# A four-layer encoder step in fp32: the first rows' projection by feature and unscaled, first weights on ScalarE's queue, the gain spread by matmuls

## The chip, the core and the metric

The kernel runs on one core of a Trainium2 chip. The metric is the device time of one execution in microseconds, given as the median of several runs; the profile is of one execution more. The core has TensorE (PE), VectorE (DVE), ScalarE (ACT), GpSimd (POOL) and SyncE (SP), which here issues the DMAs. Each engine takes its instructions in the order of the built program and waits on semaphores for the others.

## What is computed

One step of a small encoder: 512 prompt rows and 8 x 16 sample rows, so 640 rows of 1024 features, in two layers of mixer and SwiGLU. Only the first layer's beginning matters here. Its mixer starts with an RMS norm and a projection, and the columns `v` of that projection are layer-normalised:

```python
def rms_norm(x, g):
    y = x * rsqrt(mean(x * x, axis=-1) + EPS)
    return y * g
h = rms_norm(x, norm_mix_pre[0])
u, v, bg, cg, xb = split(h @ ev_w_in[0])          # five times 512 columns
vn = (v - mean(v)) * rsqrt(var(v) + EPS) * v_gain # chunk_mlp
s  = tril(W_s) @ vn + b;  ya = u * s
```

The factor `r = rsqrt(mean(x * x) + EPS)` is one number a row. So v can be projected from rows that carry only the gain g: it comes out divided by r, and its variance divided by r squared.

## The kernel before

The 640 rows are five tiles of 128 (t = 0 to 4; 4 holds the sample rows). A tile goes through these steps, of which the first four are `pre_norm` (L352) and `Quarters.take` (L317):

1. `load` (L1271 in `main`) brings the rows in, 512 KB.
2. ScalarE squares them and sums along the row, VectorE makes the mean, POOL takes the power -0.5 (`rsqrt`, L234), VectorE multiplies rows by r and by the gain tile (`SCALAR_TENSOR_TENSOR`). The gain tile is a 512 KB DMA that repeats one row in all 128 partitions (`bcast`, L200).
3. PE transposes the result: eight transposes of 128 x 128 (`flip`, L171) into two PSUM banks.
4. `take` splits the transposed tile into a high part (a cast to fp32r on ScalarE) and a low part (a subtraction on VectorE), copies of it (`f`, `a21`) to ScalarE, and the sums s1 to s4 that a later product scheme by quarters (Strassen's) needs. Tile 2 lies across the two halves and is also split into `mid`, here a `q` tile.
5. `v_proj` (L418): 24 products of 128 x 512 columns into one bank: eight k blocks, each high x high, high x low, low x high. The weights come in four loads of 512 KB (w0 to w3, `raw` tiles), each split by `operand` (L219) into a `q` tile by one cast and one subtraction of 1024 columns.
6. `v_evac` (L717): statistics of v on VectorE, r by POOL, and `vn` out of PSUM on ScalarE (`ACTIVATE vn<-ps`).

After the five tiles the mixer's other columns follow in `pairs` (L770); the first pair is done plainly (`PlainUnits`), with products of 128 x 320 columns.

All accumulators and transposes come from one pool of eight PSUM banks (`psp`, L159). A tile of this pool is written again as soon as the last reader of the one before it in its bank is done: for a pair of transposes these readers are the splits, the f copies and, for the tiles 2 to 4, the a21 copies.

What order the engines take is set in three ways. `Weave` (L48) runs the generators of the source by a clock of expected PE time, so waits written as numbers (`A1`, `A2`, the argument of `W.signal`) set the order in which instructions are written. `tc.high_priority()` marks the norm steps, so the scheduler of the tile framework draws them ahead. `Ordered` (L87) keeps ScalarE's and VectorE's instructions of the opening of `main` in program order. Each engine then runs its list strictly in order.

Of the kernel before, what the change touches and what calls it, by code (L numbers as in the profile page):

```python
# [35 lines left out]
A1 = 2000  # L36
A2 = 5000
# [68 lines left out]
def trunk_kernel(  # L106
# [48 lines left out]
    hidp = ctx.enter_context(tc.tile_pool(name="hidp", bufs=7))  # L155
# [6 lines left out]
    W = Weave()  # L162
# [25 lines left out]
    def st(n=1):  # L188
        return stp.tile([P, n], F32, tag="st", name=nm("st"))
# [16 lines left out]
    def raw():  # L206
        return rawp.tile([P, 5, 512], F32, tag="raw", name=nm("raw"))

    def fetch(srcs):

        for i, src in enumerate(srcs):
            if i % 2 == 0:
                w = raw()[:, :4, :].rearrange("p (h a) c -> p h (a c)", h=2)
                nc.sync.dma_start(out=w[:, 0, :], in_=src)
                if i + 1 < len(srcs):
                    nc.sync.dma_start(out=w[:, 1, :], in_=srcs[i + 1])
            yield w[:, i % 2, :]

    def operand(src):  # L219
        n = src.shape[-1]  # L220
        q = qp.tile([P, 2, D], F32R, tag="q", name=nm("q"))
        split((q[:, 0, :n], q[:, 1, :n]), src)
        return q
# [4 lines left out]
    def split(dst, val):  # L228
        act.copy(out=dst[0], in_=val)
        dve.tensor_tensor(out=dst[1], in0=val, in1=dst[0].bitcast(F32), op=ALU.subtract)  # L230

    def rsqrt(ms):
        r = st()
        nc.gpsimd.tensor_tensor(out=r, in0=ms, in1=mhalf, op=ALU.pow)  # L234
        return r
# [113 lines left out]
                split((self.s4[:, 0, :, o], self.s4[:, 1, :, o]), s4)  # L349
                W.signal(self.sum[t], 4500)  # L350

    def pre_norm(t, x, X, wait, xn=None):  # L352
        if xn is None:
            xn = t4([P, D])
        with tc.high_priority():
            norm = Norm()
            norm.add(x, xn)
            r = norm.get()
            dve.scalar_tensor_tensor(out=xn, in0=x, scalar=r, in1=X.gain, op0=ALU.mult, op1=ALU.mult)
        yield wait  # L360
        ps = []
        for half in range(2):
            ps.append(bank((P, HK, P)))
            for i in range(HK):
                k = HK * half + i
                flip(ps[half][:, i, :], xn[:, k * P : (k + 1) * P])
        yield 500
        X.take(t, ps)

# [45 lines left out]
                yield  # L415
        return ps[:, :n]

    def v_proj(X, hls, evac):  # L418
        for t in range(TT):
            for e in X.ready(t):  # L420
                yield e
            ps = bank()
            for k in range(NK):
                q = hls[k // 2][:, :, k % 2 * 512 : (k % 2 + 1) * 512]
                x = X.rows(k, t)
                mm(ps, x[0], q[:, 0, :], k == 0, False, 512)
                mm(ps, x[0], q[:, 1, :], False, False, 512)
                mm(ps, x[1], q[:, 0, :], False, k == NK - 1, 512)
                if k % 4 == 3:
                    yield  # L430
            evac(t, ps)
# [50 lines left out]
    def in_row(t):  # L482
        return xp[t * P : (t + 1) * P, :] if t < 4 else xs
# [224 lines left out]
        o = hist_n + NP  # L708
        return buf[:, o : o + NB * (hist_n + LS)].rearrange("p (b s) -> p b s", s=hist_n + LS)

    def even_mixer(X, hls):
        vn = {}
        vns = [hidp.tile([P, 2, NT], F32, tag="hid", name=nm("vn")) for _ in range(3)]
        consts = [t4([P, 2, 512]) for _ in range(2)]
# [2 lines left out]
        def v_evac(t, ps):  # L717
            stats = st(6)
            dve.bn_stats(out=stats, in_=ps)
            mv = st(2)  # L720
            dve.bn_aggr(out=mv, in_=stats)
            ve = st()
            dve.tensor_scalar(out=ve, in0=mv[:, 1:2], scalar1=EPS, scalar2=None, op0=ALU.add)
            r = rsqrt(ve)
            vn[t] = vns[t // 2][:, t % 2, :512]
            nm_ = st()
            dve.scalar_tensor_tensor(
                out=nm_, in0=mv[:, 0:1], scalar=-1.0, in1=r, op0=ALU.mult, op1=ALU.mult
            )
            act.activation(out=vn[t], in_=ps, func=AF.Identity, scale=r, bias=nm_)  # L730
            if t == 4:
                o = t2([P, 512])
                dve.tensor_tensor(out=o, in0=vn[t], in1=gn, op=ALU.mult)
                nc.sync.dma_start(out=nav, in_=o)
# [1 line left out]
        gn = bcast(v_gain[0], 512, lambda _: consts[0][:, 0, :])  # L736
        gcol = cst.tile([P, 4], F32, name="gcol")
        nc.sync.dma_start(out=gcol, in_=v_gain_t)
        yield from v_proj(X, hls, v_evac)
        W.signal(v_ready, 4000)  # L740

        wT = consts[1][:, 0, :].rearrange("p (g i) -> p g i", i=P)
# [3 lines left out]
        for b in range(NB):  # L746
            r = slice(b * LS, (b + 1) * LS)
            nc.sync.dma_start(out=wS[r, :, r], in_=sp_wT[0:LS, :, 0:LS])
        for g in range(4):
            for w in (wT, wS):  # L750
                nc.gpsimd.affine_select(  # L751
                    out=w[:, g, :],
                    in_=w[:, g, :],
# [509 lines left out]

    def main():
        X = Quarters(None, True)
        feed = fetch([ev_v[i] for i in range(4)])
        xt = []

        def load(t):
            xt.append(t4([P, D]))  # L1270
            nc.sync.dma_start(out=xt[t], in_=in_row(t))  # L1271

        def start(t, wait):
            g = pre_norm(t, xt[t], X, wait)
            next(g)
            W.spawn(g, 0, wait)

        Ordered.on = True
        load(0)
        X.gain = bcast(g_mix_pre[0], D, t4)  # L1280
        w = [next(feed) for _ in range(2)]
        load(1)
        w += [next(feed) for _ in range(2)]
        first = pre_norm(0, xt[0], X, 0)
        next(first)
        hls = [operand(w[0])]
        for _ in first:
            pass
        W.signal(X.top[0])
        hls.append(operand(w[1]))  # L1290
        start(1, A1)
        hls += [operand(w[2]), operand(w[3])]
        for t in range(2, TT):
            load(t)
            start(t, A1 + (t - 1) * A2)
        Ordered.on = False
        X = yield from even_mixer(X, hls)
        nxt = []

        def mid():  # L1300
            gpost = bcast(g_ffn_post[0], D, t4)
            nxt.append(Normed(bcast(g_mix_pre[1], D, t4)))
            return make_fin(gpost, x_row, x_row, nxt[0])

        yield from ffn(0, X, mid)
        X = yield from odd_mixer(nxt[0])

# [102 lines left out]
```

## Time and profile before

| | |
|---|---|
| time, median of 3 runs | 1320.69 us (1320.46 to 1320.77) |
| the profiled execution | 1320.24 us |
| its span on the core | 1318.5 us |
| PE busy | 1294.0 us, 98% |
| VectorE busy | 889.0 us, 67% |
| ScalarE busy | 614.0 us, 47% |
| first PE instruction | 8.04 us |
| first product of 320 columns (first pair) | 45.77 us |

In the timeline a row reads: start, length, engine, line of the kernel, operation, written tile <- read tiles, shape, count; in brackets how long the engine was idle before it and what released it. Times are in us from the start of the span. L167 is the line of every product, L171 of every transpose, L99 of every VectorE and ScalarE instruction, so tiles tell them apart: `q` is a split weight, `x`, `a` and mid's `q` are split rows, `ps` is a PSUM bank, `t` a 4 KB tile, `st` a small one, `raw` unsplit weights. A PE row of many products ends when the last one drains, so the rate is read from the starts of rows that follow each other.

### The profile page before, as it was taken

The numbers are of one execution on the slowest core, as the hardware profiler recorded it, in microseconds if no ns is written. First come the engines' busy times: TensorE is split into PE (matmuls) and PEld (weight loads), VectorE is DVE, ScalarE is ACT, GpSimd is POOL, SyncE is SP. The second block draws the span as 40 slices with busy tenths as digits, with TensorE's granted clock in tenths as the row PEclk, the third lists the DMA queues.
The fourth block names the chain that finished last, engine by engine and source line by source line (L and its number), as shares of the span: only waits on it lengthen the run. The fifth ranks groups of instructions, "written<-read, shape, count | busy, mean of one in ns | idle before, by whom it ended". The sixth has DMA issues, their size and how long they took to land.

```text
span 1318.5 us, 20069 instructions
## 1 busy us (share of the span) xinstructions
PE 1294.0 (98%) x8060; PEld 1178.4 (89%) x8060; DVE 889.0 (67%) x1452; ACT 614.0 (47%) x1130; POOL 54.9 (4%) x107
## 2 busy tenths in 40 slices
PE   6999999999999999999999999999999999999997
PEld 5998989989899998998799885789999898998996
DVE  6985779837576675776736556489557575864766
ACT  5644546535254352454433455366455261551551
POOL 2200101000000000000210000010000000000000
PEclk9999999999999999999999999999999999999999
DMA  7212253212223122126435336532213021230233
GB/s 249 73 65 81 96 200 138 96 48 81 96 73 120 53 77 112 64 84 218 163 120 195 147 143 250 197 128 102 107 64 128 32 98 63 96 115 30 97 128 128
DMA packets 45965, 150.12 MB, mean 114 GB/s; under 512 B 6576, under 2 KB 8496, under 8 KB 45872
## 3 DMA queue, kind: packets, MB, share of 16 engines
q1 hardware_dynamic: 45872, 148.84, 31.2%
q8 instruction: 63, 1.03, 0.3%
q14 instruction: 30, 0.25, 0.1%
HBM read 133.57 MB, written 15.26 MB: 113 GB/s over the span
## 4 chain that ended last, share of the span: by engine, by line
PE 86%; DVE 5%; issue 3%; ACT 2%; DMA 2%; POOL 1%; SPq 0%; DVEq 0%; POOLq 0%; ACTq 0%
PE ps L167 84%; DVE t L99 3%; PE ps L171 1%; DMA xbuf<-t 1%; POOL st L234 1%; ACT t L99 1%; DMA raw<-in_dram 1%; DVE q L99 1%; ACT q L99 1%; DVE x L99 1%; DVE st L99 0%; ACT ps L99 0%; ACT f L99 0%; POOL t L751 0%; SPq L380 0%
## 5 line engine op out<-in xcount | busy, mean ns | idle before, releaser
L167 PE MATMUL ps<-x,q 128*128 128x320 f32 (+2 forms) x4884 | 727.4, 309 | 1.2 <-DVE q L99 0.8
L167 PEld LDWEIGHTS ps<-x,q 128*128 128x128 f32 x4884 | 717.5, 188 | 6.2 <-issue 2.9
L167 PE MATMUL ps<-q,hid 128*128 128x512 f32 x1800 | 417.3, 391 | 0.2 <-DVE hid L99 0.2
L99 ACT CAST q<-raw 128x1024 fp32r<-128x1024 f32 (+1 forms) x278 | 269.7, 977 | 296.8 <-PE ps L167 247.1
L99 DVE TENSOR_TENSOR q<-raw,q 128x1024 fp32r<-128x1024 f32 (+1 forms) x278 | 313.9, 1132 | 134.4 <-ACT q L99 129.3
L167 PEld LDWEIGHTS ps<-q,hid 128*128 128x128 f32 x1800 | 335.5, 188 | 70.9 <-issue 1.7
L99 ACT COPY t<-ps 128x320 f32<-128x320 f32 (+2 forms) x304 | 135.0, 451 | 193.7 <-PE ps L167 173.8
L99 DVE TENSOR_TENSOR t<-ps,t 128x512 f32<-128x512 f32 (+2 forms) x164 | 100.3, 614 | 93.2 <-PE ps L167 93.0
L99 DVE TENSOR_TENSOR raw<-raw 128x512 f32<-128x512 f32 (+1 forms) x141 | 121.9, 866 | 11.6 <-DMA raw<-in_dram 10.0
L99 DVE TENSOR_TENSOR t<-t,t 128x512 f32<-128x512 f32 (+4 forms) x107 | 57.8, 551 | 48.5 <-ACT t L99 46.7
L234 POOL TENSOR_TENSOR st<-st,mhalf 128x1 f32<-128x1 f32 x45 | 31.7, 705 | 1005.9 <-DVE st L99 1001.1
L99 DVE SCALAR_TENSOR_TENSOR t<-t,st,t 128x512 f32<-128x512 f32 (+1 forms) x60 | 54.5, 925 | 16.6 <-POOL st L234 15.1
L99 ACT ACTIVATE t<-t 128x320 f32<-128x320 f32 (+1 forms) x60 | 40.1, 668 | 45.0 <-issue 26.2
L171 PE MATMUL ps<-ident,t 128*128 128x128 f32 x288 | 42.2, 281 | 12.0 <-DVE t L99 9.6
L171 PEld LDWEIGHTS ps<-ident,t 128*128 128x128 f32 x288 | 33.4, 143 | 21.9 <-DVE t L99 9.9
L99 ACT CAST hid<-t 128x320 fp32r<-128x320 f32 (+1 forms) x96 | 45.9, 482 | 11.1 <-DVE t L99 8.9
L99 DVE TENSOR_TENSOR t<-t 128x320 f32<-128x320 f32 (+3 forms) x90 | 48.8, 542 | 1.4
L99 DVE TENSOR_TENSOR hid<-t,hid 128x320 fp32r<-128x320 f32 (+1 forms) x96 | 48.8, 512 | 0.1
L167 PE MATMUL ps<-q,x 128*128 128x512 f32 x192 | 47.6, 402 | 1.2 <-DVE st L99 0.8
L99 ACT ACTIVATE ps<-t 128x512 f32<-128x512 f32 x40 | 24.1, 603 | 50.6 <-DVE t L99 50.6
L167 PEld LDWEIGHTS ps<-q,x 128*128 128x128 f32 x192 | 36.1, 192 | 10.6 <-DVE q L99 2.3
L99 DVE TENSOR_TENSOR t<-t,ps 128x320 f32<-128x320 f32 x47 | 22.9, 487 | 33.2 <-PE ps L167 33.2
(90 smaller groups left out, 497.5 us busy)
## 6 DMA issues: line engine op xcount, KB each, us to landing
raw<-in_dram SPq DMA_DIRECT2D x184, 512.0 KB, 4.1
x<-in_dram SPq DMA_DIRECT2D x24, 512.0 KB, 6.1
t<-in_dram SPq DMA_DIRECT2D x22, 512.0 KB, 5.8
xbuf<-t SPq DMA_DIRECT2D x15, 512.0 KB, 3.4
t<-xbuf SPq DMA_DIRECT2D x15, 512.0 KB, 3.9
out_dram<-t SPq DMA_DIRECT2D x15, 256.0 KB, 2.0
c<-in_dram SPq DMA_DIRECT2D x4, 512.0 KB, 4.2
fscr<-x SPq DMA_DIRECT2D x2, 768.0 KB, 3.3
```

The costliest lines, as they stand in the source:

```text
L99: ins = op(*args, **kw)
L167: nc.tensor.matmul(out, lhsT=lhsT, rhs=rhs, start=start, stop=stop, skip_group_check=more)
L171: nc.tensor.transpose(out=out, in_=in_, identity=ident)
L234: nc.gpsimd.tensor_tensor(out=r, in0=ms, in1=mhalf, op=ALU.pow)
```

## The change

Tile 0's rows come a second time, laid out by feature as `first_t` (128 features of a block by 8 blocks by 128 rows), and the gain as `first_g` (feature by block). VectorE multiplies the transposed rows by the gain, feature by feature, they are split into `top`, and tile 0's projection reads `top` instead of the normed and transposed rows. It so lacks the factor r; `v_evac` multiplies the variance by r twice before EPS is added, and the resulting factor by r. Tile 0 still goes through its norm, transposes and splits, for the mixer's other columns, but after its projection. w0 is loaded from ScalarE's queue; the other loads stand on SP's queue in a new order. The gain tile is no longer a 512 KB DMA: one row of 4 KB is loaded and two products with a row of ones spread it into two PSUM banks, from where ScalarE copies it out. Tile 1 is normed ahead of tile 0. The written waits for the tiles change: 2600 for tile 1, 7500 for tile 0, then 9500 and 6000 for each further one.

```diff
-    def pre_norm(t, x, X, wait, xn=None):
+    def pre_norm(t, x, X, wait, xn=None, scale=None, pause=False):
...
             r = norm.get()
+            if scale is not None:
+                scale.append(r)
+        if pause:
+            yield
+        with tc.high_priority():
             dve.scalar_tensor_tensor(out=xn, in0=x, scalar=r, in1=X.gain, op0=ALU.mult, op1=ALU.mult)
...
-    def v_proj(X, hls, evac):
+    def v_proj(X, hls, evac, first=None):
         for t in range(TT):
-            for e in X.ready(t):
-                yield e
+            if t or first is None:
+                for e in X.ready(t):
+                    yield e
...
-                x = X.rows(k, t)
+                if t or first is None:
+                    x = X.rows(k, t)
+                else:
+                    x = [f[:, k, :] for f in first]
...
+            var = mv[:, 1:2]
+            if t == 0:
+                var = st()
+                dve.tensor_scalar(
+                    out=var, in0=mv[:, 1:2], scalar1=scale[0], scalar2=scale[0], op0=ALU.mult, op1=ALU.mult
+                )
             ve = st()
-            dve.tensor_scalar(out=ve, in0=mv[:, 1:2], scalar1=EPS, scalar2=None, op0=ALU.add)
+            dve.tensor_scalar(out=ve, in0=var, scalar1=EPS, scalar2=None, op0=ALU.add)
             r = rsqrt(ve)
+            if t == 0:
+                own, r = r, st()
+                dve.tensor_tensor(out=r, in0=own, in1=scale[0], op=ALU.mult)
...
-        load(0)
-        X.gain = bcast(g_mix_pre[0], D, t4)
-        w = [next(feed) for _ in range(2)]
-        load(1)
-        w += [next(feed) for _ in range(2)]
-        first = pre_norm(0, xt[0], X, 0)
-        next(first)
-        hls = [operand(w[0])]
-        for _ in first:
-            pass
-        W.signal(X.top[0])
-        hls.append(operand(w[1]))
-        start(1, A1)
-        hls += [operand(w[2]), operand(w[3])]
+        nc.scalar.dma_start(out=w[0], in_=ev_v[0])
+        nc.sync.dma_start(out=xt0[:, :HK], in_=first_t[:, :HK])
+        nc.sync.dma_start(out=gt, in_=first_g)
+        nc.sync.dma_start(out=grow[0:1, :], in_=g_mix_pre[0].unsqueeze(0))
+        nc.sync.dma_start(out=xt0[:, HK:], in_=first_t[:, HK:])
+        nc.sync.dma_start(out=w[1], in_=ev_v[1])
+        xt.append(None)
+        load(1)
+        for i in (2, 3):
+            nc.sync.dma_start(out=w[i], in_=ev_v[i])
+        xt[0] = t4([P, D])
+        nc.sync.dma_start(out=xt[0], in_=in_row(0))
...
+        for i in range(2):
+            gps.append(bank())
+            nc.tensor.matmul(
+                gps[i], lhsT=ones[0:1, :], rhs=grow[0:1, i * 512 : (i + 1) * 512], start=True, stop=True
+            )
+        hls = []
+        for i in range(2):
+            c = slice(i * HK, (i + 1) * HK)
+            dve.tensor_tensor(
+                out=xt0[:, c], in0=xt0[:, c], in1=gt[:, c].unsqueeze(2).broadcast_to([P, HK, P]), op=ALU.mult
+            )
+            split((top[0][:, c], top[1][:, c]), xt0[:, c])
+            hls.append(operand(w[i]))
+            act.copy(out=X.gain[:, i * 512 : (i + 1) * 512], in_=gps[i])
+        second = pre_norm(1, xt[1], X, 2600, pause=True)
+        next(second)
+        hls.append(operand(w[2]))
+        next(second)
+        W.spawn(second, 0, 2600)
+        hls.append(operand(w[3]))
+        scale = []
+        first = pre_norm(0, xt[0], X, 0, None, scale, pause=True)
+        next(first)
+        load(2)
+        next(first)
+        W.spawn(first, 0, 7500)
         for t in range(2, TT):
-            load(t)
-            start(t, A1 + (t - 1) * A2)
+            if t > 2:
+                load(t)
+            start(t, 9500 + (t - 2) * 6000)
```

How the order of the built program moves is seen at three places. The changed kernel's lines are 2 higher in the helpers (L169 products, L173 transposes).

On ScalarE, before, from tile 0's split to tile 1's (ps23 and ps24 are tile 0's transposes, ps53 and ps54 tile 1's, ps60 tile 2's; f11 and f12 take the copies):

```order
L99 COPY f11_102<-ps23_127 128x4x128
L99 COPY f12_103<-ps24_132 128x4x128
L99 CAST q25_143<-raw15_108 128x1024
L99 ACTIVATE t4_26_146,st27_147<-t4_16_111 128x1024
L99 CAST q30_154<-raw17_113 128x1024
L99 CAST q31_157<-raw17_113 128x1024
L99 ACTIVATE t4_33_162,st34_163<-t4_32_160 128x1024
L99 CAST x2_93<-ps53_211 128x4x128
L99 CAST x3_94<-ps54_216 128x4x128
L99 COPY f11_102<-ps53_211 128x4x128
L99 CAST q1_92<-ps60_250 128x512
L99 COPY f12_103<-ps54_216 128x4x128
```

On ScalarE now, from tile 2's split into mid on (ps56 is tile 0's projection, ps57 and ps58 tile 1's transposes, ps66 and ps67 tile 0's, ps69 and ps70 tile 2's):

```order
L99 CAST q1_92<-ps69_289 128x512
L99 CAST q1_92<-ps70_294 128x512
L99 ACTIVATE t4_42_178,st43_179<-t4_41_176 128x1024
L99 CAST x2_93<-ps69_289 128x4x64
L99 CAST x3_94<-ps70_294 128x4x64
L99 ACTIVATE t4_47_188,st48_189<-t4_46_186 128x1024
L99 ACTIVATE vn51_196<-ps56_204,st65_251,st64_249 128x512
L99 COPY f11_102<-ps57_229 128x4x128
L99 COPY f12_103<-ps58_234 128x4x128
L99 COPY f11_102<-ps66_260 128x4x128
L99 COPY f12_103<-ps67_265 128x4x128
```

The four f copies of tiles 0 and 1, the last readers of four banks, stood right behind the splits of their tile; now they stand behind the squares of tiles 3 and 4 and behind vn of tile 0.

On PE, before, from tile 3's transposes on (ps67 and ps68 are tile 3's, ps79 and ps80 tile 4's, ps74 is tile 2's projection; in brackets whose semaphore an instruction waits for):

```order
L171 MATMUL ps67_316<-ident_84,t4_38_172 128x128 [waits DVE_49,PE_49]
L171 MATMUL ps67_316<-ident_84,t4_38_172 128x128 x3
L171 MATMUL ps68_321<-ident_84,t4_38_172 128x128 [waits PE_49]
L171 MATMUL ps68_321<-ident_84,t4_38_172 128x128 x3
L167 MATMUL ps74_337<-q22_124,q1_92 128x512 [waits Activation_49]
L167 MATMUL ps74_337<-q22_124,q1_92 128x512 x5
L167 MATMUL ps74_337<-q25_143,q1_92 128x512 x6
L171 MATMUL ps79_371<-ident_84,t4_43_182 128x128 [waits DVE_49,PE_49,Activation_49]
L171 MATMUL ps79_371<-ident_84,t4_43_182 128x128 x3
L167 MATMUL ps74_337<-q30_154,q1_92 128x512 [waits Activation_49]
L167 MATMUL ps74_337<-q30_154,q1_92 128x512 x2
L171 MATMUL ps80_376<-ident_84,t4_43_182 128x128 [waits Activation_49]
```

On PE now, from tile 2's transposes on (ps69, ps70; ps68 is tile 1's projection, ps80 and ps81 are tile 3's transposes, ps86 is tile 2's projection):

```order
L173 MATMUL ps69_289<-ident_84,t4_37_168 128x128 [waits DVE_49]
L173 MATMUL ps69_289<-ident_84,t4_37_168 128x128 x3
L173 MATMUL ps70_294<-ident_84,t4_37_168 128x128 x4
L169 MATMUL ps68_276<-q30_151,x3_94 128x512 [waits Activation_49]
L169 MATMUL ps68_276<-q30_151,x3_94 128x512 x5
L169 MATMUL ps68_276<-q31_155,x3_94 128x512 x6
L173 MATMUL ps80_353<-ident_84,t4_42_178 128x128 [waits Activation_49]
L173 MATMUL ps80_353<-ident_84,t4_42_178 128x128 x3
L173 MATMUL ps81_358<-ident_84,t4_42_178 128x128 [waits PE_49,Activation_49]
L173 MATMUL ps81_358<-ident_84,t4_42_178 128x128 x3
L169 MATMUL ps86_384<-q24_133,q1_92 128x512 [waits PE_49,Activation_49]
L169 MATMUL ps86_384<-q24_133,q1_92 128x512 x5
```

Tile 3's transposes waited for VectorE, which scales their rows; now they wait for ScalarE alone, though VectorE still scales those rows (t4_42): the ScalarE instruction that lets a bank go, vn51<-ps56, is itself behind that scaling. Before, the wait for vn stood ahead of the second half of tile 4's transposes (ps80), with half of tile 2's projection done; now it stands ahead of tile 3's, with all of tile 2's projection to come.

On VectorE, before, from the mean of tile 4's squares to the factors of vn of tile 0 (st55 to st59):

```order
L99 TENSOR_SCALAR st45_185<-st44_183 128x1
L99 BN_STATS st55_239<-ps52_198 128x6
L99 SCALAR_TENSOR_TENSOR t4_43_182<-t4_42_180,st46_187,t4_14_106 128x1024
L99 BN_AGGR st56_241<-st55_239 128x2
L99 TENSOR_TENSOR x4_95<-ps61_255,x4_95 128x4x64
L99 TENSOR_SCALAR st57_243<-st56_241 128x1
L99 TENSOR_TENSOR x4_95<-ps68_321,x4_95 128x4x128
L99 SCALAR_TENSOR_TENSOR st59_247<-st56_241,st58_245 128x1
```

On VectorE now, from the mean of tile 3's squares to the factors of vn of tile 0 (st59 to st65):

```order
L99 TENSOR_SCALAR st44_181<-st43_179 128x1
L99 TENSOR_TENSOR x2_93<-ps69_289,x2_93 128x4x64
L99 SCALAR_TENSOR_TENSOR t4_42_178<-t4_41_176,st45_183,t4_21_125 128x1024
L99 TENSOR_TENSOR x3_94<-ps70_294,x3_94 128x4x64
L99 TENSOR_SCALAR st49_191<-st48_189 128x1
L99 BN_STATS st59_239<-ps56_204 128x6
L99 SCALAR_TENSOR_TENSOR t4_47_188<-t4_46_186,st50_193,t4_21_125 128x1024
L99 BN_AGGR st60_241<-st59_239 128x2
L99 TENSOR_SCALAR st61_243<-st60_241,st35_163 128x1
L99 TENSOR_SCALAR st62_245<-st61_243 128x1
L99 TENSOR_TENSOR st64_249<-st63_247,st35_163 128x1
L99 SCALAR_TENSOR_TENSOR st65_251<-st60_241,st64_249 128x1
```

The statistics of tile 0's projection stand at the same kind of place, behind tile 3's and between tile 4's steps; what moved is that two small instructions are new behind them, and that PE has less done when they come.

More of the change, by code (lines that the diff above doesn't have):

```diff
@@ L135, in trunk_kernel @@
     rb_rev,
+    first_t,
+    first_g,
     yp,
@@ L709, in seg, with even_mixer @@
         return buf[:, o : o + NB * (hist_n + LS)].rearrange("p (b s) -> p b s", s=hist_n + LS)
-    def even_mixer(X, hls):
+    def even_mixer(X, hls, first, scale):
         vn = {}
@@ L738, in even_mixer @@
         nc.sync.dma_start(out=gcol, in_=v_gain_t)
-        yield from v_proj(X, hls, v_evac)
+        yield from v_proj(X, hls, v_evac, first)
         W.signal(v_ready, 4000)
@@ L1265, in main @@
         X = Quarters(None, True)
-        feed = fetch([ev_v[i] for i in range(4)])
         xt = []
@@ L1278, in main @@
         Ordered.on = True
-        load(0)
-        X.gain = bcast(g_mix_pre[0], D, t4)
-        w = [next(feed) for _ in range(2)]
-        load(1)
-        w += [next(feed) for _ in range(2)]
-        first = pre_norm(0, xt[0], X, 0)
-        next(first)
-        hls = [operand(w[0])]
-        for _ in first:
-            pass
-        W.signal(X.top[0])
-        hls.append(operand(w[1]))
-        start(1, A1)
-        hls += [operand(w[2]), operand(w[3])]
+        w = []
+        for _ in range(2):
+            r = raw()[:, :4, :].rearrange("p (h a) c -> p h (a c)", h=2)
+            w += [r[:, 0, :], r[:, 1, :]]
@@ new lines, in main @@
+        ones = cst.tile([P, P], F32, name="ones")
+        dve.memset(ones, 1.0)
+        grow = t4([P, D])
+        gt = cst.tile([P, NK], F32, name="gt")
+        xt0 = t4([P, NK, P])
+        nc.scalar.dma_start(out=w[0], in_=ev_v[0])
[4 more added lines that the diff above has]
+        nc.sync.dma_start(out=w[1], in_=ev_v[1])
@@ new lines, in main @@
+        xt.append(None)
+        load(1)
+        for i in (2, 3):
+            nc.sync.dma_start(out=w[i], in_=ev_v[i])
+        xt[0] = t4([P, D])
+        nc.sync.dma_start(out=xt[0], in_=in_row(0))
+        top = [hidp.tile([P, NK, P], F32R, tag="hid", name=nm("top")) for _ in range(2)]
+        X.gain = t4([P, D])
+        gps = []
+        for i in range(2):
[3 more added lines that the diff above has]
+            )
@@ L1293, in main @@
+        hls.append(operand(w[2]))
[4 more added lines that the diff above has]
+        first = pre_norm(0, xt[0], X, 0, None, scale, pause=True)
+        next(first)
+        load(2)
+        next(first)
+        W.spawn(first, 0, 7500)
         for t in range(2, TT):
-            load(t)
-            start(t, A1 + (t - 1) * A2)
+            if t > 2:
+                load(t)
+            start(t, 9500 + (t - 2) * 6000)
         Ordered.on = False
-        X = yield from even_mixer(X, hls)
+        X = yield from even_mixer(X, hls, top, scale)
@@ L1382 @@
         i["d_rel_bias"][:, :, ::-1],
+        i["x_prompt"][0, :P].reshape(P, NK, P).transpose(2, 1, 0),
+        i["norm_mix_pre"][0].reshape(NK, P).T,
     ]
```

## The prediction

> **What bounds the kernel now.** First the page's top, for who is busy.
>
> ```profile
> span 1318.5 us, 20069 instructions
> PE 1294.0 (98%) x8060; PEld 1178.4 (89%) x8060; DVE 889.0 (67%) x1452; ACT 614.0 (47%) x1130; POOL 54.9 (4%) x107
> ```
>
> The profiled execution took 1320.24 us, 1.74 more than its span; the median of the runs shown, 1320.69, is 0.45 above it. PE is idle for 1318.5 - 1294.0 = 24.5 us. Where, the table of busy times by stretch tells (columns: stretch, length, PE, PEld, DVE, ACT, POOL, clock, DMA share, GB/s):
>
> ```profile
> 0.00:10.00 10.00, 1.96 (x9) 1.74 (x9) 2.67 (x4) 4.06 (x5) 1.38 (x9) 1.00 0.80 281
> 10.00:35.00 25.00, 22.90 (x106) 17.24 (x106) 19.86 (x37) 17.43 (x33) 6.70 (x15) 1.00 0.61 217
> 35.00:160.00 125.00, 125.00 (x788) 119.28 (x787) 95.35 (x142) 65.63 (x104) 10.01 (x17) 1.00 0.20 74
> ```
>
> Ten of the idle microseconds lie before 35 us; from there PE is full to 160. So the start is worth what it does to the moment from which PE never waits again. The chain of waits gives that moment (start, length, what):
>
> ```profile
> 31.48 0.79 ACT vn L99
> ...
> 32.31 0.66 PE ps L171 x4
> 32.97 37.16 PE ps L167 x222
> ```
>
> PE's last wait is for the eviction of the first rows' v projection ("vn"), which ends at 32.27 and frees a PSUM bank. What PE had done by then is in the timeline (start, length, engine, line, operation, count, wait before it):
>
> ```profile
> 8.04 1.97 PE L171 MATMUL ps<-ident,t 128*128 128x128 f32 x8 [8.04 <-DVE t L99]
> 9.83 3.04 PE L167 MATMUL ps<-q,x 128*128 128x512 f32 x6
> 16.34 1.09 PE L171 MATMUL ps<-ident,t 128*128 128x128 f32 x8 [0.38 <-DVE t L99]
> 17.48 2.79 PE L167 MATMUL ps<-q,x 128*128 128x512 f32 x11
> 21.47 5.71 PE L167 MATMUL ps<-q,x 128*128 128x512 f32 x24
> 32.73 2.33 PE L167 MATMUL ps<-q,q 128*128 128x512 f32 x9
> 34.89 2.89 PE L167 MATMUL ps<-q,a 128*128 128x512 f32 x12
> 37.61 2.88 PE L167 MATMUL ps<-q,x 128*128 128x512 f32 x12
> 45.77 7.20 PE L167 MATMUL ps<-x,q 128*128 128x320 f32 x48
> ```
>
> Tile 0's projection ends at 20.27, tile 1's at 27.18. When vn is out, 4 of 40 transposes and 9 + 48 products are left, and the v projection ends at 45.77. A block of 12 products takes 37.61 - 34.89 = 2.72, so 0.227 each; a transpose 1.09 / 8 = 0.137; a product of 320 columns 7.20 / 48 = 0.15.
>
> **The change, part by part.** Its steps run on ScalarE and VectorE, at these durations:
>
> ```profile
> 0.80 1.28 ACT L99 ACT_TABLE_LOAD   x1 [0.80 <-PEq L1384]
> 0.81 0.38 SPq L1271 DMA_DIRECT2D t<-in_dram  x1
> 4.11 1.06 ACT L99 ACTIVATE t<-t 128x1024 f32<-128x1024 f32 x1 [2.03 <-DMA t<-in_dram]
> 6.70 1.28 DVE L99 SCALAR_TENSOR_TENSOR t<-t,st,t 128x1024 f32<-128x1024 f32 x1 [1.26 <-DMA t<-in_dram]
> 7.94 1.05 ACT L99 CAST q<-raw 128x1024 fp32r<-128x1024 f32 x1 [2.68 <-DMA raw<-in_dram]
> 9.02 1.23 DVE L99 TENSOR_TENSOR q<-raw,q 128x1024 fp32r<-128x1024 f32 x1 [1.04 <-ACT q L99]
> 17.04 1.07 ACT L99 CAST x<-ps 128x512 fp32r<-128x512 f32 x2
> 28.06 0.69 DVE L99 BATCH_NORM_STATS2 st<-ps 128x6 f32<-128x512 f32 x1
> 30.42 0.14 DVE L99 TENSOR_SCALAR st<-st 128x1 f32<-128x1 f32 x1
> 30.71 0.54 POOL L234 TENSOR_TENSOR st<-st,mhalf 128x1 f32<-128x1 f32 x1
> 36.54 1.42 DVE L99 TENSOR_TENSOR x<-t,x 128x256 fp32r<-128x256 f32 x4
> 47.59 1.89 DVE L99 TENSOR_TENSOR x<-t,x 128x512 fp32r<-128x512 f32 x3
> ```
>
> A square with its sum takes 1.2 (the sum's readout added). In a run of VectorE instructions one of 512 columns costs 0.60 (1.89: twice 0.60 and a last 0.69), one of 256 0.33 (1.42: thrice 0.33 and 0.42). The first 512 KB, issued at 0.81, were in use 3.3 later.
>
> *The data.* The 512 KB broadcast of the gain goes. It moved slowly:
>
> ```profile
> 3.00:4.50 1.50, 0.00 (x0) 0.00 (x0) 0.00 (x0) 0.39 (x1) 0.00 (x0) 1.00 1.06 298
> 4.50:6.00 1.50, 0.00 (x0) 0.00 (x0) 0.15 (x1) 0.76 (x2) 0.40 (x1) 1.00 0.90 218
> 9.00:10.50 1.50, 1.50 (x7) 1.09 (x5) 1.48 (x2) 1.04 (x2) 0.00 (x0) 1.00 1.02 418
> ```
>
> The DMA engines were full at 298 and 218 GB/s there, where plain tiles reach 418. Now 256 KB of transposed rows and 512 KB of weights come first. The old first 512 KB were in use at 4.11; 256 KB more at 418 GB/s make 4.7. That ScalarE's queue adds bandwidth I don't take: one queue alone filled the engines (share 1.02 in the last row). With bandwidth of its own the chain below would start 0.6 earlier and the sum be 0.6 less. [...] Everything after it (w1, row tiles 1 and 0, w2, w3, 512 KB per 1.25 us) lands by 12, two microseconds ahead of its use. The table load on ScalarE, now behind a DMA issue, takes 1.28, ends before 3 and hides behind the data.
>
> *The gain.* Two fp32 products of 512 columns, priced by
>
> ```profile
> L167 PE MATMUL ps<-t,x 128*128 128x512 f32 x8 | 4.2, 606 | 0.0
> ```
>
> at 0.53 each, or double while PE is slow (as at 8.04): 1.1 to 2.1 us on a PE that waits for data. Cost 0; uncovered at worst 2.1, which the next weights' split would take up.
>
> *First products.* Multiply by the gain 0.69 (4.7 to 5.4), cast 0.6 (6.0), cast w0 1.05: first product at 7.1, not 9.83. The rest is paced by splits: w0's low part 1.23 (8.3), second multiply 0.69 (9.0), its cast (9.6), w1's cast (10.6), half the gain out of PSUM, square of tile 1, w2's cast (13.2). VectorE then does w2's low part (14.5), tile 1's scaling 1.28 (15.7), w3's low part (16.8), and after POOL's 0.54 tile 0's scaling (17.5 to 18.8). Tile 0's projection ends at 18.1, 2.2 earlier. Tile 0's transposes follow 18.8 to 19.95, tile 1's first half to 22.7, tile 2's transposes to 23.8, the second half to 26.7: the lead has shrunk to 0.5.
>
> *The bank.* Next stand tile 3's transposes. Eight PSUM banks are held then: two projections and three pairs of transposes. Before, ScalarE copied f out of tile 0's and 1's banks at once, so four were free. Now these copies stand behind vn on ScalarE's queue, and the first bank to come free is vn's. VectorE gets to vn late: from 23.8, two casts of tile 2 (24.9), square of tile 3 (26.0), POOL (26.8), its scaling 1.28 (28.1), 0.42 of split (28.4), statistics 0.69 (29.1), tile 4's scaling 1.28 (30.4), aggregate and, newly, one more small step (30.9), POOL (31.5), two small ones (31.9), vn 0.79: **32.7**, against 32.27. The new steps, some 3.1 us of VectorE and 2.4 of ScalarE, are in this chain. PE stands from 26.7 to 32.7, and ScalarE and VectorE have nothing else to give it.
>
> *What is left then.* 16 transposes (2.2) and 72 products (16.3), not 4 and 57: the v projection ends at 51.2 if PE runs at full speed. After its first idle time PE was slow: eight transposes took 1.97 against 1.09 later, with the clock column at 1.00 in both, and products were slow to about 12.3. Half speed for 4 us loses 2.0: 53.2. [...]
>
> *The other limit.* After the projection PE's order has ten products of the first pair (1.5), then one that needs the low part of its first weights. On VectorE that stands behind tile 3's and 4's sums: a21's cast is out 2.9 after vn (four f copies, 2.1 by the row of 17.04, and three of half the width, 0.8), 35.6; then ten instructions of 256 columns (3.3), nineteen of 512 (11.4), two statistics (1.2), small ones 0.4, the split 1.23: 53.1, or 54.3 with waits between. PE would be there at 52.7 unslowed, 54.7 slowed; before, at 45.77 + 1.5 = 47.3. So the loss is 5.8 to 7.4 whichever holds. I take **7.0**: the two limits lie close, and either alone gives nearly all. From there PE's work is as before. 1320.24 + 7.0 = 1327.2 for a profiled run, **1327.7** for the median.
>
> **The rivals.** *Shorter stall* (0.10): the data come earlier, or ScalarE's instructions cost less, and vn ends 1.5 us sooner with PE not slowed: 4.0, so 1324.7. *Late rows* (0.10): tile 2's rows are queued behind 1 MB of weights, issued at 12 when w1's split frees their buffer; 3.3 for a first tile and 1.25 for each of two more make 17.8, just when ScalarE asks for them (17.9, after tile 1's split). 2 us later, all after it shifts: 9.0, so 1329.7. *Hidden* (0.04): PE's idle time is only moved, because the ends of later stages have slack: 1320.7. Against it: those idle times (24.5 less the 10.1 of the first 35 us, so 14.4) are waits for work that itself waits for PE. *Faster* (0.04): vn, or an f copy, frees a bank before PE gets to tile 3's transposes. Then PE runs on from 26.7 with 2.2 + 16.3 and ends at 45.2, 0.6 better; where the splits don't eat the lead of 2.2 either, 2.8 better: 1317.9. It decides at 26.7: each microsecond by which the first release comes later costs one. For it: tile 0's sums are ready at 18.1. Against it: VectorE's order, with ten instructions between.
>
> **How the numbers follow.** My forecast has 0.72. What a measurement of this kernel can tell from no change is about 0.2%, 2.6 us: under 1318.0 is faster, over 1323.3 slower. Slower is forecast, both sizes of stall: 0.72 + 0.10 + 0.10 = 0.92; same 0.04 and faster 0.04. The range leaves out hidden and faster, and reaches from a shorter stall with some bound to spare, 1324.3, to late rows, 1329.9.
>
> **What would show it.** PE's first v product near 7, not 9.83; a wait of PE for ACT vn of about 6 us ending near 32.7, ahead of transposes; eight transposes behind it at about 2 us if PE is slow again; the 320-column products from about 53, not 45.77. No such wait, or 320-column products before 47, and the prediction is wrong. A wait of PE for DVE q at the pair's start would say that VectorE was the limit.

## The result, and the profile after

The changed kernel takes 1330.59 us (median of 6 runs, 1330.05 to 1331.25), the kernel before 1320.66 beside it (6 runs, 1320.28 to 1320.77). The ratio is 1.0075, with a 95% interval of 1.0064 to 1.0086: slower by 9.9 us, where 7.0 was forecast. The direction and the chief cause hold; the time lies 0.7 above the range.

The page's top of the changed kernel:

```profile
span 1329.0 us, 20112 instructions
PE 1300.0 (98%) x8064; PEld 1181.3 (89%) x8064; DVE 893.6 (67%) x1459; ACT 616.2 (46%) x1134; POOL 55.4 (4%) x107
```

The span grew by 1329.0 - 1318.5 = 10.5. PE's idle time is 29.0 now, 24.5 before; its busy time grew by 6.0, of which 3.75 are the gain products and some 2.0 products at half rate (both below). Where, the same three stretches tell (columns as before: stretch, length, PE, PEld, DVE, ACT, POOL, clock, DMA share, GB/s):

```profile
0.00:10.00 10.00, 4.20 (x5) 1.66 (x6) 3.54 (x6) 3.67 (x5) 0.83 (x8) 1.00 0.82 299
10.00:35.00 25.00, 17.98 (x81) 13.98 (x80) 19.18 (x34) 15.49 (x29) 6.98 (x15) 0.92 0.59 206
35.00:160.00 125.00, 125.00 (x766) 117.81 (x766) 94.30 (x142) 65.51 (x109) 9.98 (x19) 0.99 0.20 75
```

From 10 to 35 us PE did 81 instructions where it did 106, and the clock column, 1.00 in all three stretches before, shows 0.92. In the third stretch PE is full in both kernels, but with 766 instructions against 788. The opening on PE:

```profile
5.80 3.75 PE L1325 MATMUL ps<-t,ones 1*128 1x512 f32 x4 [5.80 <-DMA t<-in_dram]
9.47 5.43 PE L169 MATMUL ps<-q,top 128*128 128x512 f32 x13
19.46 1.09 PE L173 MATMUL ps<-ident,t 128*128 128x128 f32 x8 [0.61 <-DVE t L99]
23.94 2.98 PE L169 MATMUL ps<-q,x 128*128 128x512 f32 x12
33.13 1.97 PE L173 MATMUL ps<-ident,t 128*128 128x128 f32 x8 [6.22 <-ACT vn L99]
34.75 7.17 PE L169 MATMUL ps<-q,q 128*128 128x512 f32 x24
41.77 1.03 PE L173 MATMUL ps<-ident,t 128*128 128x128 f32 x8
53.58 0.74 PE L169 MATMUL ps<-x,q 128*128 128x320 f32 x4
```

The gain products (L1325) stand ahead of the projection on PE, which so starts at 9.47. Tile 1's ends at 26.9. Then PE stands 6.22 us for vn of tile 0, as forecast; eight transposes take 1.97 where others take 1.03, and 24 products 7.17 where 5.7 is usual. The products of 320 columns start at 53.58, not 45.77: 7.8 lost.

For the further loss the passage from each mixer to its feed-forward part is the place. Before:

```profile
214.14 3.78 PE L167 MATMUL ps<-x,q 128*128 128x320 f32 x24 [0.43 <-DVE q L99]
889.47 3.80 PE L167 MATMUL ps<-x,q 128*128 128x320 f32 x24 [0.38 <-DVE q L99]
```

After:

```profile
223.27 3.78 PE L169 MATMUL ps<-x,q 128*128 128x320 f32 x24 [1.47 <-DVE q L99]
900.01 3.78 PE L169 MATMUL ps<-x,q 128*128 128x320 f32 x24 [1.47 <-DVE q L99]
```

PE's waits for VectorE's split of a weight are 1.04 and 1.09 longer. 9.13 are lost by the first of these rows (223.27 - 214.14), 10.54 by the second (900.01 - 889.47). Of the 2.7 lost behind the opening in this profile the two waits are 2.1; the other 0.6 isn't traced. PE's order is the same in both kernels there; VectorE's is not, although the diff doesn't touch these steps. The scheduler lays the whole program by its own estimate of times, and a different opening made it draw several steps of each passage in another order.

### The profile page after: what moved, and what is told of

Its sections match the earlier page's. It is cut to its first block, busy times and chain, and to the rows that moved or that the text cites. A ratio compares the mean times of both kernels' runs of the same rounds, so it can differ in the third digit from the quotient of the medians.

```text
span 1329.0 us, 20112 instructions
## 1 busy us (share of the span) xinstructions
PE 1300.0 (98%) x8064; PEld 1181.3 (89%) x8064; DVE 893.6 (67%) x1459; ACT 616.2 (46%) x1134; POOL 55.4 (4%) x107
## 3 DMA queue, kind: packets, MB, share of 16 engines
q8 instruction: 63, 1.03, 0.3%
## 4 chain that ended last, share of the span: by engine, by line
PE 85%; DVE 6%; issue 3%; DMA 2%; ACT 2%; POOL 2%; SPq 0%; DVEq 0%; POOLq 0%; ACTq 0%
PE ps L169 84%; DVE t L99 4%; PE ps L173 2%; POOL st L236 1%; DMA xbuf<-t 1%; ACT t L99 1%; DVE q L99 1%; DMA raw<-in_dram 1%; DVE x L99 0%; DVE st L99 0%; ACT q L99 0%; DMA gt<-in_dram 0%; DMA x<-in_dram 0%; ACT ps L99 0%; POOL t L772 0%
## 5 line engine op out<-in xcount | busy, mean ns | idle before, releaser
L169 PE MATMUL ps<-x,q 128*128 128x320 f32 (+2 forms) x4884 | 727.7, 310 | 3.4 <-DVE q L99 2.9
L169 PEld LDWEIGHTS ps<-x,q 128*128 128x128 f32 x4884 | 717.6, 188 | 8.4 <-DVE q L99 3.9
L169 PE MATMUL ps<-q,hid 128*128 128x512 f32 x1800 | 417.4, 391 | 0.2 <-DVE hid L99 0.2
L169 PEld LDWEIGHTS ps<-q,hid 128*128 128x128 f32 x1800 | 335.5, 188 | 71.0 <-issue 1.7
L99 ACT COPY t<-ps 128x320 f32<-128x320 f32 (+3 forms) x306 | 136.6, 452 | 195.1 <-PE ps L169 176.2
L173 PE MATMUL ps<-ident,t 128*128 128x128 f32 x288 | 42.1, 281 | 8.8 <-ACT vn L99 6.2
L173 PEld LDWEIGHTS ps<-ident,t 128*128 128x128 f32 x288 | 33.1, 143 | 19.2 <-ACT vn L99 6.6
L99 DVE TENSOR_TENSOR t<-t,ps 128x320 f32<-128x320 f32 x47 | 22.9, 488 | 32.7 <-PE ps L169 32.7
L99 ACT ACTIVATE t<-ps,st 128x512 f32<-128x512 f32 (+4 forms) x48 | 24.6, 514 | 37.0 <-DVE st L99 31.9
L169 PE MATMUL ps<-q,x 128*128 128x512 f32 x168 | 40.2, 393 | 0.7 <-DVE q L99 0.7
```

Source lines behind the costliest of these rows:

```text
L99: ins = op(*args, **kw)
L169: nc.tensor.matmul(out, lhsT=lhsT, rhs=rhs, start=start, stop=stop, skip_group_check=more)
L173: nc.tensor.transpose(out=out, in_=in_, identity=ident)
```

## The experiments

Theory at the start: the opening's loss is the bank that vn releases, and PE's slow rate behind it; the rest is VectorE's order at the mixers' ends. Rivals: VectorE's longer list sets the opening; the data and the small loads do; what is lost later follows from something else that the opening shifts. The first four runs stood beside 1320.48 of the kernel before, the next four beside 1321.02, the last four beside 1320.76. Differences below are those of the medians as they stand; since the kernel before moved by up to 0.5 between these groups, a difference across groups is good to about 0.5. As the opening's loss I give the start of the first product that reads vn less 72.17, its start before (after: 79.98, so 7.81).

**E1, the f tiles written first.** Nine tiles (two a21, two f, two `top`, three vn) want the seven places of one pool. The source writes vn of tile 0 ahead of any f; here each f gets one zero on POOL first.

```diff
         X.gain = t4([P, D])
+        for f in X.f:
+            nc.gpsimd.memset(f[:, 0, 0:1], 0.0)
```

> The changed kernel, with one zero written by POOL into each of the two f tiles at the start (overwritten later; the outputs stay). The f, a21, top and vn tiles share a pool of seven; f's first write now comes ahead of vn's, and the f copies of tiles 1 and 0 stand right behind their splits on ScalarE, ahead of vn of tile 0. Theory A (the bank is all of the opening's loss): PE's 6 us wait for vn goes, transposes of tile 3 start by 28, the 320-column products start near 45.5 instead of 53.58, the opening's loss falls from 7.8 to about 0, and with the 2.5 lost later the time is 1322 to 1323. Theory B (the bank, and right behind it VectorE's list up to the low part of the first pair's first weights): the same until 45.5, then PE waits for DVE q until about 52; the opening still loses about 4 and the time is 1326 to 1327.5. Rival C (the release of the banks is not what PE waits for; the later data and the new steps are): PE still starts tile 3's transposes at 32 or later, 1330 to 1331.

1329.55, ratio 1.0065 (1.0048 to 1.0081). ScalarE's row of tile 1's copies, and PE's rows:

```profile
20.46 1.15 ACT L99 COPY f<-ps 128x512 f32<-128x512 f32 x2
```

```profile
28.59 1.06 PE L173 MATMUL ps<-ident,t 128*128 128x128 f32 x8 [1.27 <-DVE t L99]
52.17 8.00 PE L169 MATMUL ps<-x,q 128*128 128x320 f32 x44 [2.69 <-DVE q L99]
```

In the changed kernel ScalarE has them behind vn:

```profile
32.30 0.78 ACT L99 ACTIVATE vn<-ps,st,st 128x512 f32<-128x512 f32 x1 [4.69 <-DVE st L99]
32.98 2.59 ACT L99 COPY f<-ps 128x512 f32<-128x512 f32 x6
```

The copies stand at 20.46 instead of 32.98, and no bank is missing: tile 3's transposes start at 28.59 and wait only for their rows. So the order of the first writes into that pool had put the copies behind vn. But the time fell by 1 us alone. PE arrives at the first pair early and waits 2.69 for DVE q; 44 products then take 8.00, where E4 below takes 6.71 for as many. The opening's loss is 6.09. Theory B is right on the wait and its end at 52, not on the size: the slow products behind the wait were not in it. Theory A and rival C fall.

**E2 and E3, one multiply at the mixers' ends.** Both tie the last tile's first multiply z to the scaling of tile 3: behind it in the kernel before (E2), ahead of it in the changed one (E3).

```diff
+                if (t, h) == (4, 0) and self.quarters:
+                    tc.add_manual_dep(zi.ins, scaled[0].ins.name, order_only, reason="z")
```

In E3 the last line reads `tc.add_manual_dep(scaled[0].ins, zi.ins.name, order_only, reason="z")`. `order_only` is short here for a dependence that sets the order and adds no wait; the lines that keep `scaled` and `quarters` are left out.

> The kernel before, with one change of order at the two passages from a mixer to its feed-forward part: VectorE's first multiply of the last tile's rows by the post-norm gain (z) is put behind the scaling of tile 3, as it stands in the changed kernel. Nothing is added or left out. Theory (the 1.3 and 1.15 us that the changed kernel loses at these two places come from this place in VectorE's list alone): PE waits 1.5 instead of 0.4 for DVE q at each, 2.3 to 2.5 us slower, 1323.0 to 1323.2. Rival (the loss there follows from something else that the opening shifts: transfers, the state of the queues, PE's rate): the same as before, 1320.5 to 1321.

> The changed kernel, with the same multiply put back ahead of the scaling of tile 3 at both passages, as in the kernel before. Theory: PE's waits there fall from 1.47 to about 0.4 each, 2.3 to 2.5 us faster than the changed kernel, 1328.1 to 1328.3. Rival (the place of this multiply is a symptom): 1330.6.

E2: 1321.16, ratio 1.0004 (0.9994 to 1.0013). E3: 1330.31, ratio 1.0073 (1.0058 to 1.0088). The first passage in E2 and in E3:

```profile
214.58 3.78 PE L167 MATMUL ps<-x,q 128*128 128x320 f32 x24 [0.65 <-DVE q L99]
```

```profile
224.03 3.79 PE L169 MATMUL ps<-x,q 128*128 128x320 f32 x24 [1.15 <-DVE q L99]
```

The wait moved from 0.43 to 0.65 and from 1.47 to 1.15: a fifth to a third of what was expected. This multiply is a part of the cause at most; the theory as I had put it falls.

**E4, PE kept busy.** Tile 1's 24 products are done a second time into the same bank.

```diff
+            if t == 1 and first is not None:
+                for k in range(NK):
+                    q = hls[k // 2][:, :, k % 2 * 512 : (k % 2 + 1) * 512]
+                    x = X.rows(k, t)
+                    for i, (a, b) in enumerate(((0, 0), (0, 1), (1, 0))):
+                        nc.tensor.matmul(
+                            ps, lhsT=x[a], rhs=q[:, b, :], start=k + i == 0, stop=k == NK - 1 and i == 2
+                        )
             evac(t, ps)
```

> The changed kernel, with tile 1's 24 projection products done twice into the same bank (the second time from zero, so the outputs stay): 5.5 us of extra products in the time in which PE stands and waits for vn. Theory A (PE's slow rate after the wait, 7.17 us for 24 products and 1.97 for eight transposes, is 2 us of the loss): eight transposes take 1.1, 24 products 5.7, and the time is 2.0 to 2.4 us less, 1328.2 to 1328.6. Theory B (PE's slow rate costs little, because VectorE's split of the first pair's first weights ends at 54.78, 0.3 before PE asks for it): the same faster rows, but then a wait of PE for DVE q of 1.5 to 2.3, and a time within 0.5 of 1330.6. Rival C (the rows are slow for another reason than the idle time): rows as slow as now, and the time longer by what the extra products overrun.

1330.75, ratio 1.0078 (1.0063 to 1.0093). PE's rows (L447 are the extra products):

```profile
26.56 5.60 PE L447 MATMUL ps<-q,x 128*128 128x512 f32 x24
32.93 1.13 PE L173 MATMUL ps<-ident,t 128*128 128x128 f32 x8 [0.77 <-ACT vn L99]
33.89 5.74 PE L169 MATMUL ps<-q,q 128*128 128x512 f32 x24
54.74 6.71 PE L169 MATMUL ps<-x,q 128*128 128x320 f32 x44 [1.48 <-DVE st L99]
```

The slow rows are gone, and nothing is gained: PE now stands 1.48 at the first pair. The releaser named is a small VectorE step right behind the split of the first weight (which ends at 54.69), whose low part these products read. Theory B holds. In the changed kernel itself the two limits lie 0.3 apart; VectorE ends that split at 53.59 + 1.19 = 54.78:

```profile
53.59 1.19 DVE L99 TENSOR_TENSOR q<-raw,q 128x1024 fp32r<-128x1024 f32 x1
```

In the kernel before the same split starts at 42.84, in the middle of tile 4's steps:

```profile
42.84 1.19 DVE L99 TENSOR_TENSOR q<-raw,q 128x1024 fp32r<-128x1024 f32 x1
```

There the scheduler put it ahead of tile 4's sums, in the changed kernel (and in E1) behind them.

**E5 and E6, the mixers' ends in the other kernel's order.** Some 38 VectorE and 7 ScalarE instructions at each passage are chained, without a wait, in the order that they have in the other kernel.

```diff
+        for names in ORDER:
+            for a, b in zip(names, names[1:]):
+                tc.add_manual_dep(at[b], a, order_only, reason="order")
```

`ORDER` holds four lists of instruction names, one for each engine and passage.

> The kernel before, with VectorE's and ScalarE's instructions at the two mixers' ends (some 38 on VectorE and 7 on ScalarE at each) in the order that they have in the changed kernel; all other orders, loads and numbers stay. E2 showed that the last tile's first multiply alone makes 0.25 us of each passage's loss; three more pairs of steps stand the other way round there. Theory (the whole order makes the 1.3 and 1.15 us): PE waits about 1.5 for DVE q at each, the span grows by 2.2 to 2.6, the time is 1322.6 to 1323.2. Rival (the loss there comes from elsewhere, and the order makes only what E2 showed): 0.5 to 0.9 longer than before, 1321.2.

> The changed kernel, with VectorE's and ScalarE's instructions at the two mixers' ends in the order of the kernel before. Theory: PE waits about 0.4 for DVE q at each, 2.2 to 2.6 us less than the changed kernel, 1328.0 to 1328.3. Rival: 0.5 less at most, 1330.1.

E5: 1323.00, ratio 1.0014 (1.0006 to 1.0023), 2.0 more than before. E6: 1328.23, ratio 1.0052 (1.0038 to 1.0066), 2.4 less than the changed kernel. PE at the two passages in E5, then in E6:

```profile
215.33 3.78 PE L167 MATMUL ps<-x,q 128*128 128x320 f32 x24 [1.47 <-DVE q L99]
891.84 3.79 PE L167 MATMUL ps<-x,q 128*128 128x320 f32 x24 [1.46 <-DVE q L99]
```

```profile
221.88 3.78 PE L169 MATMUL ps<-x,q 128*128 128x320 f32 x24 [0.42 <-DVE q L99]
897.54 3.79 PE L169 MATMUL ps<-x,q 128*128 128x320 f32 x24 [0.45 <-DVE q L99]
```

The waits change places to a few hundredths, with either opening. So the order alone makes this loss. How, VectorE's waits for POOL show; in E5, ahead of the first passage:

```profile
197.85 1.42 DVE L99 SCALAR_TENSOR_TENSOR t<-t,st,t 128x512 f32<-128x512 f32 x2 [0.73 <-POOL st L234]
201.72 1.28 DVE L99 SCALAR_TENSOR_TENSOR t<-t,st,t 128x1024 f32<-128x1024 f32 x1 [0.44 <-POOL st L234]
205.66 1.42 DVE L99 SCALAR_TENSOR_TENSOR t<-t,st,t 128x512 f32<-128x512 f32 x2 [0.73 <-POOL st L234]
210.27 1.28 DVE L99 SCALAR_TENSOR_TENSOR t<-t,st,t 128x1024 f32<-128x1024 f32 x1 [0.40 <-POOL st L234]
```

and in the kernel before:

```profile
197.11 1.42 DVE L99 SCALAR_TENSOR_TENSOR t<-t,st,t 128x512 f32<-128x512 f32 x2 [0.44 <-POOL st L234]
204.68 1.41 DVE L99 SCALAR_TENSOR_TENSOR t<-t,st,t 128x512 f32<-128x512 f32 x2 [0.72 <-POOL st L234]
```

VectorE stands 2.30 us for POOL's powers in one order and 1.16 in the other, where multiplies of other tiles fill that time. The difference, 1.1, is about what PE waits longer. E2 had moved one of these multiplies only.

**E7 and E8, the first pair's splits early.** The low parts of its two weights are put ahead of tile 4's first sum and behind it, about where the kernel before has them; E7 is E1 with this, E8 is E4 with this. The edit is a chain like that of E5, of five VectorE instructions.

> E1 (f first), with the low parts of the first pair's two weights put on VectorE where the kernel before has them, the first ahead of tile 4's sums, the second behind the first of these sums. Theory B (with the bank free, the place of this split behind tile 4's sums is the opening's limit): PE's wait of 2.7 for DVE q goes, with it the slow products behind it (44 in 8.0 us against 6.7 in other runs), 3.5 to 4.2 us less than E1, 1325.3 to 1326.0. Rival D (VectorE as a whole is late; moving the split ahead only makes tile 4's sums late): a new wait behind the first pair of about the same size, 1328.5 to 1329.5.

> E4 (tile 1's products done twice, PE not slow after its wait), with the same two splits early. Theory: PE's slow rate costs 2 us as soon as VectorE isn't behind it; the 1.5 us wait at the first pair goes, 1328.9 to 1329.4. Rival D: the wait moves, 1330.5 to 1331.

E7: 1325.06, ratio 1.0028 (1.0018 to 1.0039). E8: 1329.20, ratio 1.0059 (1.0046 to 1.0072). E7's split on VectorE, and the row of PE that waited for it in E1:

```profile
46.52 1.20 DVE L99 TENSOR_TENSOR q<-raw,q 128x1024 fp32r<-128x1024 f32 x1
```

```profile
47.97 6.76 PE L169 MATMUL ps<-x,q 128*128 128x320 f32 x45
```

No wait and no slow products: 4.5 us less than E1 (4.2 at most were expected), the opening's loss is 1.76. Moving the split costs nothing that PE sees, so rival D falls. E8 has PE at full rate (24 products in 5.74, as in E4) and no wait at the first pair: it takes 1.5 us less than E4, about the wait of 1.48 there, and 1.4 less than the changed kernel, though in its profile vn came 0.5 later.

**E9, all orders put back.** E7 with E6's chains at the mixers' ends.

> E7 (f first, the first pair's splits early) with the mixers' ends in the order of the kernel before, as in E6. Theory (the two causes are independent and add): E7 less the 2.3 of E6, 1322.5 to 1323.0, and about 1.8 above the kernel before, all of it ahead of the first products of 320 columns, because tile 0's projection doesn't start early enough to pay for the new steps. Rival (the losses overlap, since the mixers' ends have slack that a later opening uses up): 1324 to 1325.

1322.51, ratio 1.0013 (1.0004 to 1.0021): E7 less 2.6. The two causes add. What is left is 1.75, and the opening's loss is 2.10. One row shows a part of it:

```profile
28.90 1.06 PE L173 MATMUL ps<-ident,t 128*128 128x128 f32 x8 [1.79 <-DVE t L99]
```

Tile 3's transposes wait 1.79 for their scaled rows, which stand on VectorE behind the steps that the change added. That these steps are all of the 1.75 no run isolates.

**E10 and E11, the small loads first.** E10 is E9, E11 the changed kernel, with this edit:

```diff
-        nc.sync.dma_start(out=xt0[:, :HK], in_=first_t[:, :HK])
         nc.sync.dma_start(out=gt, in_=first_g)
         nc.sync.dma_start(out=grow[0:1, :], in_=g_mix_pre[0].unsqueeze(0))
+        nc.sync.dma_start(out=xt0[:, :HK], in_=first_t[:, :HK])
```

> E9 with the two loads of 4 KB (the gain by feature, the gain's row) issued ahead of the first transposed rows instead of behind them. In the changed kernel they land at 5.5, and the multiply by the gain and the two gain products wait for them. Theory 1 (they set the start): the multiply starts near 4.7, the gain products at 3 to 4, the first product of the projection at 7 to 8 instead of 9.3, and the projection of tile 0 ends 0.6 to 0.9 earlier: 1321.6 to 1322.3. Theory 2 (the splits of the later weights set the projection's end): the first product earlier, the time as E9 within 0.3.

> The changed kernel, with only these two small loads moved ahead. Theory 1: the first product at 7 to 8, vn of tile 0 and the release of its bank 0.5 to 0.8 earlier, the time 0.5 to 0.8 less than the changed kernel's, 1329.7 to 1330.0. Theory 2: vn's end within 0.2 of 33.1, the same time, 1330.5.

E10: 1322.87, ratio 1.0019 (1.0010 to 1.0029). E11: 1330.68, ratio 1.0079 (1.0066 to 1.0091). E11 is as without the edit; E10 is 0.4 longer, with runs from 1321.8 to 1325.4. E11's first product, and its row behind the wait:

```profile
7.98 0.80 PE L169 MATMUL ps<-q,top 128*128 128x512 f32 x1
...
33.03 1.97 PE L173 MATMUL ps<-ident,t 128*128 128x128 f32 x8 [6.18 <-ACT vn L99]
```

The first product comes 1.5 us earlier, vn 0.1. Theory 2 holds as far as this goes: the splits of the later weights pace tile 0's projection. But the earlier multiply that Theory 1 counts on did not come about, because it now waits for the rows. VectorE's first multiply by the gain in the changed kernel, then in E11:

```profile
5.58 0.69 DVE L99 TENSOR_TENSOR t<-t,gt 128x512 f32<-128x512 f32 x1 [4.52 <-DMA gt<-in_dram]
```

```profile
5.46 0.69 DVE L99 TENSOR_TENSOR t<-t,gt 128x512 f32<-128x512 f32 x1 [4.39 <-DMA t<-in_dram]
```

From this multiply to the end of w3's low part are 11.8 us in both (to 17.38 and to 17.27). So the two runs show that an earlier PE gains nothing; they don't show what earlier rows would gain. In E10's one profile the opening's loss fell to 1.00, but the median of 11 runs didn't follow; I count nothing for it. Nor did that execution itself: at the second passage PE is 0.15 ahead of E9's profile (891.69 against 891.84), where it was 1.10 ahead in the opening. No run isolates where that was lost again.

**E12, w0 on SP's queue.**

```diff
-        nc.scalar.dma_start(out=w[0], in_=ev_v[0])
+        nc.sync.dma_start(out=w[0], in_=ev_v[0])
```

> The changed kernel, with w0 issued first on SP's queue instead of on ScalarE's. All else stays. If a second issuing queue gave bandwidth of its own, the first rows and weights would come 0.6 us later here and the time be 0.6 longer, 1331.1; if it only saves an issue of 0.4 us, 0 to 0.4 longer, 1330.5 to 1330.9; if the two first loads disturb each other on two queues, up to 0.5 shorter.

1330.70, ratio 1.0078 (1.0066 to 1.0091). The queue makes no difference to the time that can be measured. Its profile speaks against bandwidth of its own: the multiply by the gain starts at 5.13 here, and between 5.39 (E4) and 5.97 (E1) in the runs with w0 on ScalarE's queue and the small loads in the same places; the first product of the projection comes at 9.49, against 9.47 in the changed kernel. The prediction took no such bandwidth either.

No version beats the kernel before; E9 comes nearest.

## Why the prediction was right and wrong

**Right: the bank.** The wait of 6 us for vn, its place ahead of tile 3's transposes and what was left behind it came as worked out: vn ends at 33.09 (32.7 forecast). Only why the copies stood behind vn was missing: E1 shows that the order of first writes into the pool did it.

**The rival "late rows"** came in part. ScalarE waits for tile 2's rows, but PE doesn't: their transposes start at 23.15, where 22.7 was forecast.

```profile
19.13 1.06 ACT L99 ACTIVATE t<-t 128x1024 f32<-128x1024 f32 x1 [0.81 <-DMA t<-in_dram]
```

**Right: the slow rate.** From 33.13 to 53.58, where the v projection is done, are 20.45 us. In E4 the same work runs from 32.93 to 51.63, with two early products of the pair (0.29) in between: 18.4. So 2.0 were lost, as the term said. The stretch itself was longer than the term had it: 4.75 us of work at half rate (last section), not 4, and half of that is 2.4.

**Right: two limits that lie close.** PE would ask for the split at 55.1 and VectorE had it at 54.78. E1 took away PE's wait for the bank and E4 its slow rate, and neither gained more than 1.0; E7 and E8 removed VectorE's as well and gained 5.5 and 1.4. The split came 0.5 behind the later end of its forecast, 53.1 to 54.3.

**Mis-sized: the opening, 7.0 taken and 7.8 measured.** 0.4 is vn, late by the chain on VectorE; 0.4 is that 7.0 was taken out of 5.8 to 7.4, where the upper end came about, with PE slowed and ready for the pair at 53.2 by the forecast, 53.58 measured.

**Wrong at the start, with little effect.** The first data were in use at 5.58, not 4.7; the gain products took 3.75 (four instructions of 1.06 each; the row that priced them has 606 ns), not 2.1 at worst; the first product started at 9.47, not 7.1. The price of the gain products was read wrongly: 0.53 is the price of one instruction in the profile, and the two products of the source are four instructions (L1325 x4), so 2.1 at that price and 4.2 at twice that. E11, with its first product 1.5 earlier, shows that the gain products don't reach the time, so "cost 0" stands by its result and not by its price. For the first data it shows nothing, as its multiply came only 0.1 earlier. The profiles hint that they reach vn: the multiply starts at 5.13 (E12), 5.46 (E11), 5.58 and 5.85 (E3), and vn ends at 32.93, 32.98, 33.09 and 33.49. So the 0.9 by which the first data were late may be behind the 0.4 of vn; that is not shown.

**The step that failed: "From there PE's work is as before."** PE's work was, VectorE's order was not. 2.0 (E5) to 2.4 (E6; 2.7 if each is taken from the kernel before beside it) of the 2.9 us between forecast and result were lost at two passages 200 and 890 us into the program, which the diff doesn't touch. With 7.8 and these the sum is 9.8 to 10.5, against a measured 9.9. The rival "hidden" was wrong too: between 80 and 196 us the loss stayed at 7.8.

**Open.** The 1.75 that E9 keeps, beyond the row shown; and why the scheduler drew the mixers' ends otherwise.

## What to carry to other kernels

Where a scheduler lays the whole program, compare the built order of every engine to the end, not only around the edit: a changed opening can cost 2 us in passages that nobody touched. Where a wait is to go, ask what stands next on the other engines: here PE and one split on VectorE were 0.3 us apart, and taking away a wait of 6 us on PE alone gave 1.0. When tiles of several kinds share a pool, look at which is written first; one zero written early into each of two tiles moved four copies by 10 to 12 us.

## What the runs showed of the hardware

In and behind PE's wait for vn, in E1 for VectorE's split, the clock column stood at 0.50 for some microseconds. In the changed kernel, stretches of 1 us (PE's idle time began at 26.9, its work again at 33.13):

```profile
31.00:32.00 1.00, 0.00 (x0) 0.00 (x0) 0.30 (x3) 0.00 (x0) 0.85 (x3) 0.53 0.09 13
...
36.00:37.00 1.00, 1.00 (x3) 0.74 (x3) 0.63 (x2) 1.00 (x4) 0.00 (x0) 0.50 0.00 0
37.00:38.00 1.00, 1.00 (x4) 0.77 (x3) 0.85 (x2) 1.00 (x3) 0.00 (x0) 0.56 0.00 0
```

The stretches from 32 to 37 show 0.50, those before 31 and after 38 show 1.00. If the clock goes from the one to the other at once, which is my estimate, a mean of 0.53 puts the fall at 31.06, and 0.56 the return at 37.88: 6.82 us at half rate, 4.75 of them with work. The work shows the same: eight transposes took 1.97 in it and 1.03 behind it. In E1, whose wait was 2.69 (49.5 to 52.17):

```profile
51.00:52.00 1.00, 0.00 (x0) 0.00 (x0) 1.00 (x1) 0.04 (x1) 0.00 (x0) 0.81 0.00 0
...
55.00:56.00 1.00, 1.00 (x8) 1.00 (x8) 0.56 (x3) 0.24 (x1) 0.53 (x1) 0.99 0.88 307
```

The same reckoning gives 51.62 to 55.02, 3.40 us, half of 6.82. So a wait of 2.69 had the slow stretch behind it; E9's of 1.79 had not (clock 1.00 from 25 to 35 us). What sets its start and its length no run isolates. How much work falls into the slow stretch differs between kernels whose opening is nearly the same. E12, whose PE works again at 32.98, and E11, at 33.03:

```profile
29.00:30.00 1.00, 0.00 (x0) 0.00 (x0) 0.94 (x2) 0.00 (x0) 1.00 (x3) 0.50 0.05 4
...
35.00:36.00 1.00, 1.00 (x4) 0.77 (x4) 0.28 (x1) 1.00 (x5) 0.10 (x1) 0.59 0.12 45
```

```profile
32.00:33.00 1.00, 0.00 (x0) 0.00 (x0) 0.95 (x3) 0.80 (x2) 0.00 (x0) 0.57 0.10 8
...
38.00:39.00 1.00, 1.00 (x3) 0.78 (x3) 1.00 (x4) 0.47 (x2) 0.00 (x0) 0.52 0.00 0
```

The half rate lasts from 29.00 to 35.82 and from 32.14 to 38.96, 6.82 both times, with 2.8 and 5.9 us of work in it; it was 4.75 in the changed kernel and 2.85 in E1. By this estimate it lasts 3.40 us in E1 and 6.82 in the other three, and it begins 2.1 (E1) to 5.3 us (E11) after PE has stopped.
